# One whole gate column moved from behind the fourth pair of input products to between the second and the third

## The chip, the cores and the metric

The kernel runs on one core of one Trainium2 chip. The metric is the device time of one execution in microseconds (us); lower is better. Engines are called as the profile calls them: PE (TensorE, matrix products), DVE (VectorE), ACT (ScalarE), POOL (GpSimd), SP (SyncE, which here only issues DMAs).

## The reference, cut to what matters

One decoder layer over 1024 positions of width 1024, float32. `hybrid_mixer` is the part in which the change lies:

```python
def hybrid_mixer(u, w_in, conv_w, conv_norm_g, ret_norm_g, w_out):
    z = u @ w_in                                   # (1024, 1024) @ (1024, 3584)
    cb, cc, ch = jnp.split(z[..., :c0], 3, axis=-1)        # conv group, 512 channels each
    rq, rk, rv, rg = jnp.split(z[..., c0:], 4, axis=-1)    # retention, 4 heads x 128
    y_conv = cb * causal_dwconv3(cc * ch, conv_w)
    y_conv = group_rms_norm(y_conv, conv_norm_g, CONV_GROUPS)
    ...
    o = chunkwise_retention(q, k, v).reshape(b, s, RET_WIDTH)
    y_ret = group_rms_norm(o, ret_norm_g, RET_HEADS) * jax.nn.silu(rg)
    return jnp.concatenate([y_conv, y_ret], axis=-1) @ w_out

def reference(x, ...):
    h = h + hybrid_mixer(rms_norm(h, norm1_g), ...)
    h = h + sq_relu_mlp(rms_norm(h, norm2_g), w_up, w_down)
    return rms_norm(h, final_norm_g)
```

## The kernel before, in words

Channels lie on the partitions, positions on the free axis, in two halves of 512 (`hs`). Every float32 product is made of three products of rounded numbers: a weight piece `r` (128x512) is split into a high part `wh` (an ACT cast) and a low part `wl` (a subtraction on DVE or POOL), and an activation likewise into `uh`, `ul` (or `U`, `yh`, `yl`). One product of 128 output channels by 512 positions over 512 inputs is 12 matmuls (line 403, in `mm`).

`w_in` is worked through in column tiles of 128, numbered by `f`. 0 to 11 belong to the convolution (`f // 3` is its group of channels, `f % 3` is 0 for `cc`, 1 for `ch`, 2 for `cb`), 12 to 19 are the q and k columns, 20 to 23 the four gates `rg`, one for each head. The q and k tiles come first. Then `IN_TURNS` says in which turns the others are made, and `IN_END` which come last:

```python
IN_TURNS = [0, 1, 2, 3, 20, (4, 5), (6, 7), (8, 9), (10, 11), 21]
IN_END = [22, 23]
```

- A number is a *whole* turn (`whole`, by `tile_in`): two PSUM banks at once, one for each half, and 48 matmuls that alternate between the two banks. When they are done, DVE empties both; for a gate it multiplies by `R` (the norm of the row), ACT takes the Silu, and DVE multiplies by the head's output `o_n` (this is `gate`).
- A tuple is a *pair* (`pair_in`): two column tiles by both halves, made with seven products instead of eight (Strassen's scheme), in the order `UP_ORDER = (1, 2, 5, 6, 3, 7, 4)`, each 12 matmuls in one bank. Products 1, 2 and 3 read `uh`/`ul`, the others the sums `U`. Product 1 is copied out by ACT; DVE adds the others together: one add for product 2, two for 6, one for 3, two for 7, one for 4. The bank of product 5 is read by the second add of product 6 and again by that of 7. For each pair POOL or DVE also makes four sums of weight pieces (`r<-r,r`).
- `IN_END` makes gates 22 and 23 with four banks that are all taken at the start; the order is 22 first half, 23 first half, 22 second half, 23 second half, each 24 matmuls in one bank. The output product with `w_out` follows and reads `yh`, `yl` of all eight channel tiles.

There are 8 PSUM banks: four in the pool `pm` (whole turns, products 1, 5, 3, 4 of a pair, `IN_END`) and four in `pr` (products 2, 6, 7, and the norms). A bank goes to the next tile in the order in which they were given up. The banks of product 1 and of product 3 of a pair are the two that the next tiles of `pm` get.

Four result tiles (`o` of heads 2 and 3, `y` of groups 0 and 1) are stored to DRAM early (`put_by`, line 872) and fetched back (`get_back`, line 877) at a fixed place of the loop over `IN_TURNS`, line 894:

```python
    for at, turn in enumerate(IN_TURNS):
        if isinstance(turn, tuple):
            pair_in(turn)
        else:
            whole(turn)
        if at == len(IN_TURNS) - 2:
            for h in (2, 3):
                force(("by", ("o", h)))
                o_n[h, 0] = o_n[h, 1] = get_back(("o", h))
            for i in range(2):
                force(("by", ("y", i)))
                y[i] = get_back(("y", i))
```

The rest of the convolution and of the gates (`conv_h`, `conv_b`, `norm`, `gate`, `split_y`) runs as small tasks between the products. At the time of writing the program, a planner (`background`) keeps a clock for each engine from fixed costs (the class `Engine`, line 74 in the profile for all that it issues) and one `SLOT` of 2.72 us for every 12 matmuls; by these it decides behind which product a step is written and, where two engines could do it, whether POOL or DVE does. What it decides is fixed in the program; on the chip each engine works through its own list in order. `norm` of a convolution tile writes two matmuls into PE's list (lines 483 and 484), which read the tile `s` of ACT and that of DVE or POOL. Weight pieces are split four ahead (`prepare`, four buffers each of `r`, `wh` and `wl`): a new `wh` can be cast only when PE is done with the piece four before, and a new piece is fetched (line 162) only when the split of the one four before it has been done. So SP's list, on which all these fetches and line 877 stand, waits for the splits.

The MLP, which is two thirds of the time, comes behind all this and its code is not touched.

Of the kernel before, what the change touches and what calls it, by code (L numbers as in the profile page):

```python
# [36 lines left out]


IN_QK = [12, 13, 16, 17, 14, 15, 18, 19]
IN_TURNS = [0, 1, 2, 3, 20, (4, 5), (6, 7), (8, 9), (10, 11), 21]  # L40
IN_END = [22, 23]
SLOT, LOOK, PE_MARGIN, LATE = 2.72, 3.2, 1.2, 0.0
WARM = 10
# [36 lines left out]
def hybrid_layer(  # L80
# [107 lines left out]
    IN_ORDER = list(IN_QK)  # L188
    for turn in IN_TURNS + IN_END:
        IN_ORDER += turn if isinstance(turn, tuple) else [turn]  # L190
# [37 lines left out]
    ahead = 3  # L228
    for turn in IN_TURNS + IN_END:
        if isinstance(turn, tuple):  # L230
# [191 lines left out]
    def spawn(gen, ready=None, late=0.0):  # L422
        Task(gen, now[0] if ready is None else ready, late).go()
# [39 lines left out]
    def force(key):  # L463
        while key not in got:
            background(1e9)
            assert key in got, key
# [276 lines left out]
    def whole(f):  # L743
        def evac(z):
            if f < 20 and f % 3 == 0:
                out = a_of[f // 3] = unit(s="a")
                for half, sl in enumerate(hs):
                    act.copy(out[:, sl], z[half])
                return
            out = None if f < 20 and f % 3 == 1 else unit(s="z")  # L750
            for half in range(2):
                spawn(use(f, half, out, z[half], True), clock[dve])

        tile_in(evac)
# [68 lines left out]
    def pair_in(fs):  # L823
        out = [unit(s="z") for _ in range(2)]
        (c11, c12), (acc, c22) = ([o[:, sl] for sl in hs] for o in out)
        for at, n in enumerate(UP_ORDER):
            if not got.get("pairs") and n in (5, 6, 7, 4):
                for j in range(4):
                    force(({5: "t1", 6: "t2", 7: "t3", 4: "t4"}[n], j))
            b = product(n, (pm, pr)[at % 2])  # L830
            slot()
            prepare()
            ready = None
            if n == 1:
                act.copy(acc, b)
            if n == 2:
                dve.tensor_add(c11, acc, b)
                ready = 0, 0
            if n == 5:
                b5 = b  # L840
            if n in (6, 7, 4):
                dve.tensor_add(acc, acc, b)
            if n == 6:
                dve.tensor_add(c12, acc, b5)
            if n == 7:
                dve.tensor_add(c22, acc, b5)
                ready = 1, 1
            if n == 3:
                dve.tensor_add(c12, c12, b)
                ready = 0, 1  # L850
            if n == 4:
                ready = 1, 0
            if ready:
                f, half, o = fs[ready[0]], ready[1], out[ready[0]]
                if f < 20 and f % 3 == 0:
                    a_of[f // 3] = o
                else:
                    spawn(use(f, half, o, o[:, hs[half]], False), clock[dve], LATE * half)
            tick()
        got["pairs"] = now[0]  # L860
# [5 lines left out]
    def put_by(key, of, *ready):  # L866
        for r in ready:
            yield r
        yield (dve,)
        t = of()  # L870
        spilt[key] = spill.tile([P, T], F32, tag="sp", name=nm("sp"))
        nc.sync.dma_start(spilt[key], t)
        mark(("by", key), dve)

    def get_back(key):
        t = unit(s="back")
        nc.sync.dma_start(t, spilt.pop(key))
        return t
# [13 lines left out]
    for i in range(2):  # L892
        spawn(put_by(("y", i), lambda i=i: y[i], ("y", i, 0), ("y", i, 1)))
    for at, turn in enumerate(IN_TURNS):
        if isinstance(turn, tuple):
            pair_in(turn)
        else:
            whole(turn)
        if at == len(IN_TURNS) - 2:
            for h in (2, 3):  # L900
                force(("by", ("o", h)))
                o_n[h, 0] = o_n[h, 1] = get_back(("o", h))
# [3 lines that stand above are left out]
                got["back", i] = now[0] + 10.0  # L906
# [656 lines left out]
```

## Time and profile before

| | before |
|---|---|
| device time, median of 3 runs (lowest to highest) | 1080.27 us (1080.08 to 1080.79) |
| the profiled execution's own time | 1081.81 us |
| its span | 1079.0 us |
| mean granted clock of PE | 0.997 |
| busy share of the span: PE, DVE, ACT, POOL | 98%, 81%, 43%, 50% |

The span is the time from the first to the last instruction that the profile holds. The times in a timeline are microseconds from the span's start. A number in brackets at the end of a timeline's row is the idle time of that engine ahead of the row, and what ended it; the profile gives all engine instructions that the planner issues the line of its helper, L74, so they are told apart by the names of their tiles.

### The profile page before, as it was taken

The page shows a single profiled execution, that of the slowest core. Times are in us where ns is not written, and L with a number is a line of the kernel's source. Part 1 is how long each engine was busy: PE and PEld are TensorE (multiplying, and loading weights), DVE is VectorE, ACT ScalarE, POOL GpSimd, SP SyncE. Part 2 cuts the span into 40 slices and gives each one's busy share as a digit, 9 for nine tenths or more (in the row PEclk, how much of TensorE's full clock was granted, in tenths as well). Part 3 has the DMA queues.
Part 4 walks back from the last instruction along what each step waited for, and adds up shares of the span by engine and source line. Part 5 has one row for each costly group of instructions (what it writes and reads, how often), then busy time and mean ns, then how long its engine had stood idle before and what let it go on. Part 6 is the DMA issues. An engine that isn't in the chain of part 4 may idle for free.

```text
span 1079.0 us, 13854 instructions
## 1 busy us (share of the span) xinstructions
PE 1060.5 (98%) x4860; PEld 881.6 (82%) x4860; DVE 878.7 (81%) x1246; ACT 460.2 (43%) x904; POOL 538.0 (50%) x366
## 2 busy tenths in 40 slices
PE   9999999999989999999999999999999999999997
PEld 7888888887768888788788888888888888888886
DVE  7446546799998656699999989989899899899955
ACT  8211445663435544444433443433343344334453
POOL 6234223255753223559538358267276185384552
PEclk9999999999999999999999999999999999999999
DMA  7111122222223635050121211201301301200204
GB/s 274 62 59 39 40 70 78 75 79 73 78 59 118 215 104 188 1 195 21 48 88 39 69 49 49 79 30 57 90 21 50 98 20 50 88 20 20 69 30 156
DMA packets 39685, 82.25 MB, mean 76 GB/s; under 512 B 4544, under 2 KB 5696, under 8 KB 39616
## 3 DMA queue, kind: packets, MB, share of 16 engines
q1 hardware_dynamic: 39328, 80.85, 23.0%
q8 instruction: 38, 0.62, 0.2%
q10 hardware_dynamic: 288, 0.52, 0.1%
q14 instruction: 31, 0.25, 0.1%
HBM read 71.92 MB, written 9.44 MB: 75 GB/s over the span
## 4 chain that ended last, share of the span: by engine, by line
PE 79%; DVE 10%; POOL 4%; issue 3%; ACT 2%; DMA 1%; DVEq 0%; SPq 0%; POOLq 0%; ACTq 0%
PE b L403 46%; PE b L1276 22%; PE b L357 4%; PE b L1385 4%; DVE wl L74 2%; DVE z L74 2%; POOL z L74 1%; POOL r L74 1%; DVE t L74 1%; DVE x L74 1%; DVE U L74 1%; DVE q L74 1%; DVE xs L74 1%; ACT h L74 1%; DVE m L74 1%
## 5 line engine op out<-in xcount | busy, mean ns | idle before, releaser
L403 PE MATMUL b<-U,wh 128*128 128x512 f32 x1024 | 315.8, 390 | 1.8 <-DVE x L74 1.1
L74 ACT CAST wh<-r 128x512 fp32r<-128x512 f32 x286 | 175.9, 620 | 321.2 <-PE b L403 134.5
L74 DVE TENSOR_TENSOR wl<-r,wh 128x512 fp32r<-128x512 f32 x251 | 231.8, 926 | 91.4 <-ACT wh L74 90.5
L74 POOL TENSOR_TENSOR r<-r,r 128x512 f32<-128x512 f32 x136 | 209.9, 1546 | 116.3 <-DVE wl L74 65.6
L1276 PE MATMUL b<-V,wh 128*128 128x512 f32 x784 | 242.0, 389 | 0.5 <-POOL V L74 0.4
L403 PEld LDWEIGHTS b<-U,wh 128*128 128x128 f32 x1024 | 191.8, 188 | 42.6 <-issue 1.9
L74 DVE TENSOR_TENSOR x<-x,b 128x512 f32<-128x512 f32 (+1 forms) x312 | 195.6, 673 | 30.2 <-PE b L1385 14.2
L403 PE MATMUL b<-U,wl 128*128 128x512 f32 x512 | 199.5, 390 | 0.3 <-POOL wl L74 0.3
L1276 PEld LDWEIGHTS b<-V,wh 128*128 128x128 f32 x784 | 147.1, 188 | 32.3 <-POOL V L74 0.8
L74 POOL TENSOR_TENSOR t<-t,t 128x512 f32<-128x512 f32 x70 | 106.4, 1524 | 97.9 <-ACT t L74 51.9
L1276 PE MATMUL b<-V,wl 128*128 128x512 f32 x392 | 152.5, 389 | 0.0
L74 POOL TENSOR_TENSOR wl<-r,wh 128x512 fp32r<-128x512 f32 x35 | 48.6, 1394 | 160.7 <-ACT wh L74 153.5
L403 PEld LDWEIGHTS b<-U,wl 128*128 128x128 f32 x512 | 96.2, 188 | 21.2 <-POOL wl L74 0.7
L403 PE MATMUL b<-uh,wh 128*128 128x512 f32 x304 | 103.4, 399 | 2.3 <-DVE z L74 2.3
L403 PE MATMUL b<-uh,wl 128*128 128x512 f32 x304 | 100.8, 391 | 1.1 <-DVE wl L74 1.1
L403 PE MATMUL b<-ul,wh 128*128 128x512 f32 x304 | 101.0, 392 | 0.0
L1276 PEld LDWEIGHTS b<-V,wl 128*128 128x128 f32 x392 | 73.5, 188 | 15.2
L74 POOL TENSOR_TENSOR V<-t,V 128x512 fp32r<-128x512 f32 x35 | 49.6, 1416 | 67.3 <-ACT V L74 67.3
L74 DVE TENSOR_TENSOR t<-t,b 128x512 f32<-128x512 f32 x112 | 75.8, 677 | 1.7 <-POOL t L74 1.2
L74 ACT ACTIVATE t<-t 128x512 f32<-128x512 f32 x64 | 40.2, 631 | 79.8 <-DVE t L74 79.2
L74 DVE TENSOR_TENSOR V<-t,V 128x512 fp32r<-128x512 f32 x63 | 70.3, 1116 | 0.0
L403 PEld LDWEIGHTS b<-uh,wl 128*128 128x128 f32 x304 | 57.3, 189 | 13.9 <-DVE wl L74 1.5
(178 smaller groups left out, 1422.1 us busy)
## 6 DMA issues: line engine op xcount, KB each, us to landing
r<-w_up_t SPq DMA_DIRECT2D x64, 256.0 KB, 2.6
r<-w_down_t SPq DMA_DIRECT2D x56, 256.0 KB, 2.7
r<-w_in_t SPq DMA_DIRECT2D x48, 256.0 KB, 2.7
xt<-xT SPq DMA_DIRECT2D x16, 256.0 KB, 5.4
xs<-xT SPq DMA_DIRECT2D x8, 512.0 KB, 4.9
r<-w_out_t SPq DMA_DIRECT2D x16, 256.0 KB, 2.7
x<-xT SPq DMA_DIRECT2D x8, 512.0 KB, 8.9
k<-x SPq DMA_DIRECT2D x6, 512.0 KB, 3.2
```

The source lines that it names most:

```text
L74: return f(out, *args, **kw)
L357: nc.tensor.matmul(vb[i], a[k][:, i * P : (i + 1) * P], b[k // 2][:, vs], start=(k == 0 and a is uh and b is vh), stop=(k == KT - 1 and a ...
L403: nc.tensor.matmul(b, a[:, k, :], rhs(n, k)[r], start=(start and i == 0), stop=(stop and i == len(ops) - 1),)
L1276: nc.tensor.matmul(b, a, r, start=(i == 0), stop=(i == len(ops) - 1))
L1385: nc.tensor.matmul(z, a, b, start=(k == 0 and t == 0), stop=(k == 3 and t == 2))
```

## The change

Gate column 21 is made right behind the pair (6, 7), ahead of (8, 9). The number of turns is the same, and the weights are fetched in the new order. The fetch from DRAM still stands behind the pair (10, 11), which is now the last turn, and `IN_END` follows it directly.

```diff
-IN_TURNS = [0, 1, 2, 3, 20, (4, 5), (6, 7), (8, 9), (10, 11), 21]
+IN_TURNS = [0, 1, 2, 3, 20, (4, 5), (6, 7), 21, (8, 9), (10, 11)]
...
-        if at == len(IN_TURNS) - 2:
+        if at == len(IN_TURNS) - 1:
             for h in (2, 3):
                 force(("by", ("o", h)))
                 o_n[h, 0] = o_n[h, 1] = get_back(("o", h))
```

The planner decides anew from there on. What stands in the lists of the engines at three places, before and after, follows. In these rows a name's number tells tiles apart: `b` is a PSUM bank's tile, `z` and `a` are result tiles, `cv` the convolution, `q_617` and `q_618` the outputs of heads 0 and 1.

PE, the turn that follows the pair (10, 11), before: `b_2860` is product 4 of the pair, `b_2895` and `b_2896` are the two banks of the whole turn 21, and the second of them had belonged to product 3 of the pair.

```order
L403 MATMUL b_2860<-U_2224,wh_2774 128x512 x2
L403 MATMUL b_2860<-U_2224,wl_2775 128x512
L403 MATMUL b_2895<-uh_157,wh_2807 128x512
L403 MATMUL b_2896<-uh_157,wh_2807 128x512
L403 MATMUL b_2895<-ul_165,wh_2807 128x512
```

And after: `b_2929` is product 4 of the same pair, and `b_2965` the first bank of `IN_END`, which had belonged to product 1 of that pair.

```order
L403 MATMUL b_2929<-U_2224,wh_2843 128x512 x2
L403 MATMUL b_2929<-U_2224,wl_2844 128x512
L403 MATMUL b_2965<-uh_157,wh_2876 128x512
L403 MATMUL b_2965<-ul_165,wh_2876 128x512
L403 MATMUL b_2965<-uh_157,wl_2877 128x512
```

Two banks within two instructions have become one; the next one (`b_2968`, formerly product 3) is asked for 24 matmuls later. Behind the pair (6, 7) the whole turn 21 now asks for two at once.

DVE, the stretch behind the last add of the pair (6, 7) (the first row of each), before, where the pair (8, 9) follows:

```order
L74 TENSOR_TENSOR z_2361<-z_2361,b_2512 128x512
L74 SCALAR_TENSOR_TENSOR r_2486<-b_2478,r_2486 128x512
L74 TENSOR_TENSOR wl_2551<-r_2379,wh_2550 128x512
L74 SCALAR_TENSOR_TENSOR z_2200<-z_2200,less_g,r_2485 128x512
L74 SCALAR_TENSOR_TENSOR z_2200<-r_2486,z_2200 128x512
L74 TENSOR_TENSOR wl_2575<-r_2405,wh_2574 128x512
L74 TENSOR_TENSOR z_2535<-z_2536,b_2561 128x512
```

And after, where the whole turn 21 (`z_2610` and the two `q_618`) stands between:

```order
L74 TENSOR_TENSOR z_2361<-z_2361,b_2516 128x512
L74 TENSOR_TENSOR z_2360<-z_2360,ssq 128x512
L74 TENSOR_TENSOR z_2360<-z_2360,z_2361 128x512
L74 SCALAR_TENSOR_TENSOR cv_2556<-z_2360,sm,cv_2556 128x512 x2
L74 SCALAR_TENSOR_TENSOR cv_2556<-z_2360,sm,cv_2556 128x511
L74 SCALAR_TENSOR_TENSOR cv_2556<-z_2360,sm,cv_2556 128x510
L74 TENSOR_TENSOR z_2610<-b_2540,R 128x512
L74 TENSOR_TENSOR z_2610<-b_2541,R 128x512
L74 SCALAR_TENSOR_TENSOR q_618<-z_2610,sm,q_618 128x512 x2
L74 TENSOR_TENSOR wl_2653<-r_2448,wh_2652 128x512
L74 TENSOR_TENSOR z_2617<-z_2618,b_2639 128x512
```

The convolution of group 2 (`cv`), which stood among the adds of the pair (8, 9), now stands ahead of them, in the time of turn 21; three of its four products that POOL made are DVE's now (two of them are the same row twice and shown once).

SP, around the four fetches from DRAM (`back`), before:

```order
L162 DMA r_2851<-w_out_t 128x512
L162 DMA r_2873<-w_out_t 128x512
L877 DMA back_2887<-sp_1991 128x1024
L877 DMA back_2889<-sp_1993 128x1024
L877 DMA back_2891<-sp_2221 128x1024
L877 DMA back_2893<-sp_2584 128x1024
L162 DMA r_2929<-w_out_t 128x512
```

And after:

```order
L162 DMA r_2920<-w_out_t 128x512
L162 DMA r_2942<-w_out_t 128x512
L877 DMA back_2956<-sp_1991 128x1024
L877 DMA back_2958<-sp_1993 128x1024
L877 DMA back_2960<-sp_2221 128x1024
L877 DMA back_2962<-sp_2537 128x1024
L162 DMA r_3084<-w_out_t 128x512
```

They stood behind the second piece of `w_out`, whose buffer had held the second piece of gate 22. They now stand behind the fourth, whose buffer held the second piece of gate 23. On ACT, the Silu and the reciprocal root of the norm belong to different tables: before, one change of table stands between the pair (10, 11) and the end of `IN_END`; after, three stand there.

## The prediction

> **What bounds the kernel now.** I read the page first, then the busy time in stretches around the change, then the timelines of PE, DVE, ACT and SP there.
>
> ```profile
> span 1079.0 us, 13854 instructions
> PE 1060.5 (98%) x4860; PEld 881.6 (82%) x4860; DVE 878.7 (81%) x1246; ACT 460.2 (43%) x904; POOL 538.0 (50%) x366
> PE 79%; DVE 10%; POOL 4%; issue 3%; ACT 2%; DMA 1%; DVEq 0%; SPq 0%; POOLq 0%; ACTq 0%
> ```
>
> PE is busy for 98%, and PE's own work makes 79% of the chain that ended last. The change leaves the number of matmuls as it is, so it can only win or lose PE's idle or slowed time. The stretches below are cut at PE's borders: pair (6, 7); pair (8, 9) with a norm; pair (10, 11) with a norm; turn 21 with two norms; `IN_END`.
>
> ```profile
> core 0: us, PE busy (x) PEld busy (x) DVE busy (x) ACT busy (x) POOL busy (x), PEclk, DMA share, GB/s
> 254.41:276.66 22.25, 20.91 (x90) 16.36 (x88) 20.98 (x22) 11.77 (x19) 15.52 (x11) 1.00 0.17 48
> 276.66:298.23 21.57, 20.36 (x87) 15.99 (x86) 21.23 (x23) 6.75 (x12) 14.75 (x10) 1.00 0.23 73
> 298.23:318.36 20.13, 19.80 (x87) 16.06 (x86) 18.93 (x20) 8.64 (x15) 14.29 (x10) 1.00 0.21 60
> 318.36:334.26 15.90, 13.59 (x53) 10.81 (x52) 12.61 (x18) 5.65 (x10) 4.34 (x3) 0.89 0.50 171
> 334.26:356.02 21.76, 21.76 (x97) 18.02 (x96) 17.50 (x23) 12.38 (x22) 6.52 (x4) 1.00 0.17 53
> ```
>
> `IN_END` has 96 matmuls in 21.76 us and nothing to wait for: 0.2267 us each. At that pace a pair (84) takes 19.04, turn 21 (48) 10.88, a norm (2) 0.45. So the four stretches lose: pair (6, 7), with two norms, 22.25 - 19.95 = 2.30; pair (8, 9) 21.57 - 19.49 = 2.08; pair (10, 11) 20.13 - 19.49 = 0.64; turn 21 15.90 - 11.79 = 4.11. What the change can reach is the last three: 6.8 us. In two of the four DVE is busy nearly throughout (20.98 of 22.25, 21.23 of 21.57).
>
> ```profile
> 267.03 0.50 PE L403 MATMUL b<-uh,wl 128*128 128x512 f32 x1 [1.12 <-DVE wl L74]
> ...
> 295.80 0.40 PE L403 MATMUL b<-U,wl 128*128 128x512 f32 x1
> 297.17 0.50 PE L483 MATMUL b<-s,blkr 128*128 128x512 f32 x1 [0.97 <-ACT s L74]
> 297.89 0.50 PE L484 MATMUL b<-s,blkr 128*128 128x512 f32 x1 [0.23 <-DVE s L74]
> ...
> 307.13 0.50 PE L484 MATMUL b<-s,blkr 128*128 128x512 f32 x1 [0.33 <-DVE r L74]
> ...
> 318.36 0.39 PE L403 MATMUL b<-uh,wh 128*128 128x512 f32 x1
> 321.06 0.79 PE L403 MATMUL b<-uh,wh 128*128 128x512 f32 x1 [2.31 <-DVE z L74]
> 321.65 1.05 PE L403 MATMUL b<-ul,wh 128*128 128x512 f32 x2
> ...
> 324.21 0.69 PE L403 MATMUL b<-ul,wh 128*128 128x512 f32 x2
> ```
>
> The 4.11 have two parts. Turn 21's second matmul, into its second bank, starts 321.06 - 318.36 - 0.23 = 2.47 us late, behind an add of DVE. Then seven matmuls take 324.21 - 321.06 = 3.15 us in place of 1.59: a slow clock (0.89 over the stretch) that costs 1.56.
>
> ```profile
> 272.44 2.19 DVE L74 TENSOR_TENSOR z<-z,b 128x512 f32<-128x512 f32 x3
> ...
> 281.94 0.68 DVE L74 TENSOR_TENSOR z<-z,b 128x512 f32<-128x512 f32 x1
> ...
> 283.14 0.68 DVE L74 TENSOR_TENSOR wl<-r,wh 128x512 fp32r<-128x512 f32 x1
> ...
> 287.13 1.77 DVE L74 TENSOR_TENSOR wl<-r,wh 128x512 fp32r<-128x512 f32 x1
> ...
> 318.82 2.19 DVE L74 TENSOR_TENSOR z<-z,b 128x512 f32<-128x512 f32 x3
> ...
> 327.66 0.68 DVE L74 TENSOR_TENSOR z<-z,b 128x512 f32<-128x512 f32 x1
> ```
>
> I call it DVE's lag how long after a pair's end on PE its last add (of product 4) begins. Behind (6, 7) it is 281.94 - 276.66 = 5.3 us, behind (10, 11) 327.66 - 318.36 = 9.3. The third add of the row at 318.82 is that of product 3, whose bank turn 21 gets: it ends at 321.01, and PE goes on at 321.06. The lag is the cause.
>
> ```profile
> L74 ACT CAST wh<-r 128x512 fp32r<-128x512 f32 x286 | 175.9, 620 | 321.2 <-PE b L403 134.5
> ...
> L74 POOL TENSOR_TENSOR r<-r,r 128x512 f32<-128x512 f32 x136 | 209.9, 1546 | 116.3 <-DVE wl L74 65.6
> ...
> L74 POOL TENSOR_TENSOR wl<-r,wh 128x512 fp32r<-128x512 f32 x35 | 48.6, 1394 | 160.7 <-ACT wh L74 153.5
> ```
>
> **The change part by part.** *The bank wait goes (2.47 and 1.56).* Behind (6, 7) turn 21 asks for the same pair of banks, but the add of product 3 there is the third of the row at 272.44 and done by 274.63, 2.0 us before PE arrives at 276.66; up to it the lists of PE and DVE hold the same work. `IN_END` asks for one bank (product 1, emptied by ACT long before) and for the next (product 3) only 24 matmuls, 5.4 us, later. With a lag up to 9 that is in time. Both terms to nought: 4.0, with the rest of the stretch 4.11.
>
> *The waits in the two pairs (2.08 and 0.64).* They hang on the lag. From the last add of (6, 7) to that of (10, 11) DVE had 46 instructions in 327.66 - 281.94 = 45.72 us, 0.994 each. After, it has 50 between the same two adds (the evacuation and the gate of 21 come in, four; three of POOL's products; others went to POOL). PE needs 10.88 + 2 x 19.49 = 49.86 for what lies between. At the old mean 50 take 49.7: the lag stays at 5.1 and no longer grows. That is one bound. For the other I went through the new lists by hand, 0.6 us (start to start) for an instruction of DVE that reads a bank or runs while POOL rests, 1.7 for one that meets POOL's (the two `wl` rows show both), 1.3 to 1.7 for one of POOL (rows of the page, above; their means are 1.39 and 1.55), 0.62 for a cast of ACT. The last add of (6, 7) comes at 282.9, since three SBUF instructions meet POOL; the banks of 21 are emptied by 292.7, its Silu done by 293.4, behind which ACT has the `wh` of product 3 of (8, 9), whose `wl` POOL then ends at 295.4 (PE comes for it at 298.9); the `s` tile for the first norm at 300.8 (PE: 303.9); the lag is 4.5 behind (8, 9) and 1.8 behind (10, 11). No wait of PE is left on that walk. So these two stretches keep between 0 and 2.72, the latter if they wait as before, and up to 4.6 if both do as (6, 7) did, with a lag like the first bound. I take 0.8, near the walk, whose margins are 3 us.
>
> *The end of the mixer (nothing, from below nothing to 4 us).* Turn 21 no longer covers what follows the last pair: 15.90 us less between the last pair and `w_out`. By the new list the norm of the last group stands 48 matmuls behind the pair (10.9 us), its two halves of `y` and the four tiles from DRAM must be split before `w_out`.
>
> ```profile
> 327.26 1.85 SPq L877 DMA_DIRECT2D back<-sp x4
> ...
> DMA to landing us min/median/max: 3.7/7.0/8.2
> ```
>
> ```profile
> 331.62 0.69 DVE L74 TENSOR_TENSOR s<-t,s 128x512 fp32r<-128x512 f32 x1 [0.64 <-ACT s L74]
> ```
>
> ```profile
> 334.01 0.69 ACT L74 ACTIVATE r<-b,eps 128x512 f32<-128x512 f32 x1 [0.24 <-PE b L484]
> ...
> 335.98 0.64 ACT L74 ACTIVATE r<-r 128x512 f32<-128x512 f32 x1
> 336.63 1.28 ACT L74 ACT_TABLE_LOAD   x1
> 337.93 1.15 ACT L74 ACTIVATE z<-z 128x512 f32<-128x512 f32 x2
> ```
>
> From the pair's end: the split of gate 23's second piece waits for product 4 and takes a cast and 1.7 of POOL, so SP goes on at 2.4; it issues one piece and the four fetches by 4.8; they land by 4.8 + 8.2 = 13.0. ACT's list then holds the cast of the last fetched tile (0.6), a table (1.28), four roots (2.6), a table (1.28), a Silu and the first `wh` of `w_out` (0.6 each): 20.0. POOL's `wl` is done at 21.3. PE, with `IN_END` (21.76) and two norms (0.9), asks for it at 23.1. Margin 1.8 us: cost nothing, and what lies beyond the margin would be paid one for one. The norm's own `s` is ready 332.31 - 327.66 = 4.65 behind the last add, so with a lag below 6.2 PE doesn't wait there either.
>
> The Trainium skill, "ScalarE: Activation LUTs", What ACT_TABLE_LOAD costs, speaks against the change: it puts a switch of table at 2.66 us, a load of 1.28 and a drain of 1.38. Here the load is 1.28 and its neighbours stand 0.02 us off, so no drain shows. By the page the two switches would add 2.8 us to that list, 1.0 beyond the margin, and the time would be 1075.3 (an estimate).
>
> *The rest of SP's list* (the `x` tiles, line 942) stands relative to the end of `IN_END` as before, and the MLP's lists are unchanged; it is only moved ahead.
>
> **Sum.** 4.11 + 2.72 - 0.8 = 6.0 us: span 1079.0 to 1073.0, that execution's own 1081.81 to 1075.8. It lay 1.5 above the median, so on the median 1080.27 - 6.0 = 1074.3.
>
> **The rivals.**
> *A, the pairs go on waiting.* For it: (6, 7) lost 2.30 with a lag of 5.3 at its end; the average holds 5.1. Then 4.11 is won and up to 4.6 - 2.72 = 1.9 of it given back: 1076.2 to 1078.1. Against it: the walk.
> *B, the slow clock isn't the wait's doing* but falls somewhere anyway: 1.56 stays, 1075.8. The waits of 1.12 and 0.97 were followed by no slow matmuls, the one of 2.31 was, which speaks against it. The Trainium skill, "TensorE: Matmul & The Clock Gate", What's actually happening, has the clock fall after an idle window of some 3.4 us; 2.31 is less, so by that rule B would stand.
> *C, the wait moves to the start of `w_out`.* If the fetches go out as late behind the last pair as before (327.26 - 318.36 = 8.9 in place of 2.8), they land at 18.9, the first `wl` is done at 27.3, PE waits 4.2 and pays the slow clock, 1.56, too: 0.2 won, 1080.1. Against it: SP waited then for splits that stood behind 9 us of lag.
> *D, DVE falls further behind, slower.* It got four more instructions, and among them three of POOL's. If the lag behind (10, 11) reached 12, the norm's `s` would be ready at 16.7, PE waiting 5.8 in `IN_END`, with 1.56 of slow clock and the 2.72 of the pairs as before: 10.1 lost against 6.8, 1083.5. It is slower by over 0.2% from a lag of 11 on. Against it: 10.88 more PE time for four more instructions.
>
> **How the numbers follow.** 0.2% (2.2 us) is about what a measurement here can tell from no change. The forecast (0 to 1.8 us kept, 1073.4 to 1075.3): 0.60; A 0.14; B 0.05; C 0.11; D 0.10. Faster is the forecast, A and B, 0.79; the same 0.11; slower 0.10. The best is all 6.8 and the scatter of the runs, 0.5: 1072.9; the upper end is A's worst, 1078.1; C and D, 0.21, lie beyond, and some of C (a wait of 2 us, 1076) within.
>
> **What would show it.** In the profile after: no wait of PE for an add at the start of a turn from 276 to 350; a granted clock of 1.00 there; DVE's last add within 5 us of the end of (10, 11); the four fetches issued within 5 us of it; `w_out` begun at about 350 in place of 356.02. The prediction is wrong if PE waits for `s` in `IN_END`, for `wl` at the first matmul of `w_out`, or if DVE's lag is above 6 at the end of the last pair.

## The result, and the profile after

| | before | after |
|---|---|---|
| median of the runs shown with the changed kernel (4 and 4) | 1080.17 us | 1072.45 us |
| ratio, with its 95% interval | | 0.994 (0.9926 to 0.9953) |
| median of the repetition (23 and 6 runs) | 1078.94 us | 1072.87 us |
| ratio, with its 95% interval | | 0.9943 (0.993 to 0.9957) |
| the profiled execution's span and own time | 1079.0, 1081.81 us | 1070.6, 1073.52 us |

The change makes the kernel 6.1 us faster by the repetition, which has the most runs of before; the first comparison gave 7.7. The forecast was 6.0 us, 1074.3 against 1080.27; the first median, 1072.45, lies even under the best that the prediction named, 1072.9.

The page of the kernel after: the span, the busy time of the engines, the chain that ended last by engine.

```profile
span 1070.6 us, 13856 instructions
PE 1056.1 (99%) x4860; PEld 879.3 (82%) x4860; DVE 877.7 (82%) x1249; ACT 465.3 (43%) x908; POOL 534.0 (50%) x363
PE 90%; DVE 5%; issue 1%; ACT 1%; POOL 1%; DMA 0%; DVEq 0%; SPq 0%; ACTq 0%; POOLq 0%
```

PE has the same 4860 matmuls; its share of the chain rose from 79% to 90%, DVE's fell from 10% to 5%. The stretches, cut at PE's borders in the new order: pair (6, 7); turn 21; pair (8, 9) with a norm; pair (10, 11) with a norm; `IN_END` with two norms.

```profile
core 0: us, PE busy (x) PEld busy (x) DVE busy (x) ACT busy (x) POOL busy (x), PEclk, DMA share, GB/s
251.91:274.24 22.33, 20.92 (x90) 16.36 (x88) 21.03 (x24) 11.79 (x19) 14.34 (x10) 1.00 0.23 71
274.24:285.12 10.88, 10.88 (x50) 9.01 (x48) 10.66 (x11) 2.78 (x5) 7.97 (x6) 1.00 0.12 48
285.12:304.61 19.49, 19.49 (x87) 16.14 (x86) 17.10 (x19) 10.28 (x16) 12.18 (x9) 1.00 0.16 55
304.61:324.10 19.49, 19.49 (x87) 16.14 (x86) 17.73 (x23) 7.82 (x14) 8.94 (x7) 1.00 0.27 81
324.10:346.77 22.67, 22.67 (x101) 18.77 (x100) 19.69 (x28) 16.39 (x26) 5.15 (x4) 1.00 0.33 117
```

Four of the five lose nothing: PE is busy for the whole of each, and 10.88, 19.49, 19.49 and 22.67 (21.76 and two norms, 0.91) are the lengths that the prediction had worked out for stretches without a wait. The clock is 1.00 throughout. Only (6, 7) keeps its loss, 22.33 - 19.95 = 2.38 us. The end of the mixer, on DVE (the last add and the norm's `s`), SP, POOL, PE and ACT:

```profile
328.75 0.68 DVE L74 TENSOR_TENSOR z<-z,b 128x512 f32<-128x512 f32 x1
...
332.71 0.69 DVE L74 TENSOR_TENSOR s<-t,s 128x512 fp32r<-128x512 f32 x1
```

```profile
328.35 2.07 SPq L877 DMA_DIRECT2D back<-sp  x4
```

```profile
344.58 1.48 POOL L74 TENSOR_TENSOR wl<-r,wh 128x512 fp32r<-128x512 f32 x1 [16.64 <-ACT wh L74]
```

```profile
334.98 0.39 PE L483 MATMUL b<-s,blkr 128*128 128x512 f32 x1
...
335.66 0.39 PE L484 MATMUL b<-s,blkr 128*128 128x512 f32 x1
...
346.77 0.39 PE L403 MATMUL b<-yh,wh 128*128 128x512 f32 x1
...
347.22 0.39 PE L403 MATMUL b<-yh,wl 128*128 128x512 f32 x1
```

```profile
333.74 1.28 ACT L74 ACT_TABLE_LOAD   x1
...
338.17 1.28 ACT L74 ACT_TABLE_LOAD   x1
...
341.42 0.63 ACT L74 ACTIVATE r<-r 128x512 f32<-128x512 f32 x1
342.07 1.28 ACT L74 ACT_TABLE_LOAD   x1
343.36 0.63 ACT L74 ACTIVATE z<-z 128x512 f32<-128x512 f32 x1
```

The lag behind (10, 11) is 328.75 - 324.10 = 4.65 us. The norms' four matmuls begin at 334.98; the last tile `s` that they need, DVE's for the second half, is ready at 333.40, and the fourth of them (L484) takes it at 335.66: 2.3 us to spare. The first `wl` of `w_out` is done at 344.58 + 1.48 = 346.06, PE takes it at 347.22: 1.2 us to spare.

**Where the 8.4 us between the two first traces lie.** Both have the same matmul of (6, 7) behind a wait for `wl` (at 267.03 before, quoted in the prediction), and the first matmul of `w_out`. With the two further traces of before and one of after that were taken below:

| | before, 1st | before, 2nd | before, 3rd | after, 1st | after, 2nd |
|---|---|---|---|---|---|
| start of the span to that matmul | 267.03 | 264.53 | 264.73 | 264.61 | 264.33 |
| from it to the first of `w_out` | 88.99 | 87.32 | 88.89 | 82.16 | 82.17 |
| from there to the end of the span | 722.9 | 723.8 | 723.3 | 723.9 | 724.0 |

The change's part is the middle row: 88.99 - 82.16 = 6.8 us. The 2.4 us ahead of it are not the change's, since two other traces of before start as those of after do. Most of them lie in the first microseconds: in the first 12 us of the span PE does 36 matmuls in the first trace of before, 45 and 44 in the other two, and 46 and 48 in those of after. The trace of `bank` below, 38 matmuls, starts as late. The MLP (last row) gives back 0.0 to 1.0 us, within what it varies from trace to trace.

### The profile page after: what moved, and what is told of

It reads as the page before. It is cut to its first block, busy times and chain, and to the rows that moved or that the text cites. A ratio compares the mean times of both kernels' runs of the same rounds, so it can differ in the third digit from the quotient of the medians.

```text
span 1070.6 us, 13856 instructions
## 1 busy us (share of the span) xinstructions
PE 1056.1 (99%) x4860; PEld 879.3 (82%) x4860; DVE 877.7 (82%) x1249; ACT 465.3 (43%) x908; POOL 534.0 (50%) x363
## 4 chain that ended last, share of the span: by engine, by line
PE 90%; DVE 5%; issue 1%; ACT 1%; POOL 1%; DMA 0%; DVEq 0%; SPq 0%; ACTq 0%; POOLq 0%
PE b L403 56%; PE b L1276 23%; PE b L357 4%; PE b L1385 4%; DVE wl L74 1%; DVE t L74 1%; DVE x L74 1%; DVE q L74 1%; PE b L339 0%; DVE V L74 0%; PE b L625 0%; PE b L595 0%; ACT h L74 0%; PE b L663 0%; PE b L627 0%
## 5 line engine op out<-in xcount | busy, mean ns | idle before, releaser
L74 DVE TENSOR_TENSOR wl<-r,wh 128x512 fp32r<-128x512 f32 x247 | 227.2, 922 | 86.3 <-ACT wh L74 85.6
L74 POOL TENSOR_TENSOR wl<-r,wh 128x512 fp32r<-128x512 f32 x39 | 56.3, 1448 | 166.3 <-ACT wh L74 158.8
```

What stands on the lines that cost most here:

```text
L74: return f(out, *args, **kw)
```

## The experiments

The theory is the prediction's: DVE's lag behind PE at a pair's end makes all these waits, and a whole turn, which gives DVE little to do for 10.9 us of PE, makes the lag up if it stands between the pairs. The rival: turn 21 behind the last pair asked for two banks at once, one of them product 3's, and that request alone was the cost. "Stretch" is the middle row of the table above.

| run | edit | median us | against before | stretch | lag behind (10, 11) |
|---|---|---|---|---|---|
| after_again | the changed kernel | 1072.87 | 0.9943 (0.993 to 0.9957) | 82.17 | 4.63 |
| bank | before, other bank | 1078.60 | 0.9994 (0.9985 to 1.0003) | 87.33 | 9.27 |
| relief | before, DVE less | 1075.18 | 0.9963 (0.9949 to 0.9977) | 84.67 | 7.57 |
| first | 21 behind (4, 5) | 1078.32 | 0.9994 (0.9984 to 1.0003) | | 8.03 |
| third | 21 behind (8, 9) | 1075.26 | 0.9963 (0.995 to 0.9977) | 84.31 | 4.72 |
| half | after, 7 adds more | 1077.05 | 0.998 (0.997 to 0.9991) | 84.47 | 8.56 |
| load | after, 14 adds more | 1080.19 | 1.0012 (1.0003 to 1.0021) | 89.38 | 11.82 |
| early | after, fetches earlier | 1073.01 | 0.9941 (0.9923 to 0.9959) | 82.18 | 5.22 |
| twenty | after, 20 behind (4, 5) | 1083.69 | 1.0046 (1.0033 to 1.006) | | 3.85 |

The runs were made in three groups, on three chips, and before ran beside each: 1078.94 us (after_again, bank, first, third), 1079.17 (relief, load, twenty) and 1079.14 (half, early). A comparison across groups is good to about these 0.2 us. `first` and `twenty` have no entry under stretch, since their matmuls come in another order there. The changed kernel again, without an edit:

> The changed kernel once more, to see what of its gain is the change's. In the two profiles shown so far the span fell by 8.4 us, of which 6.8 lie in the mixer and 2.4 ahead of the first difference in any list (the first matmuls start 0.6 us earlier and run faster). Theory 1: those 2.4 us are a scatter of the start, met by both kernels; the span from the same matmul to the same matmul behind the change (from the pair (6, 7)'s begin to the first matmul of w_out) falls by 6.8 again, and the medians differ by 6 to 8 us. Theory 2: the start differs from kernel to kernel; then this run starts like the first run of the changed kernel and the kernel before like its first run, and they are again 8 us apart.

The second trace of after starts as late as the first (264.33 and 264.61) and has the same stretch. The medians differ by 6.1 us, and the start is a scatter that before has too: theory 1.

**bank.** The kernel before, with the second bank of turn 21 from the other pool.

```diff
-    def tile_in(evac):
+    def tile_in(evac, second=None):
...
-        out = [bank() for _ in hs]
+        out = [bank(), bank(second)]
...
-        tile_in(evac)
+        tile_in(evac, pr if f == 21 else None)
```

> The kernel before with nothing moved: the second bank of turn 21 is taken from the other pool, so that it is not the one of product 3 of the pair (10, 11). The lists of all engines keep their order. Theory 1 (the wait of turn 21 is the wait for that bank, and the slow clock is its consequence): 2.31 us of wait and 1.56 of slow matmuls go, the stretch of turn 21 falls from 15.9 to 11.9 us, the waits in the pairs (8, 9) and (10, 11) stay; 4.0 us faster, 0.9963 of before. Theory 2 (DVE's lag of 9 us holds PE up wherever it comes next): PE waits at the next place instead, for product 3's bank in the gates 22 and 23 or for s of the norm, and less than 1 us is won. Theory 3 (the slow clock is not the wait's doing): 2.4 us faster, with a granted clock below 0.95 somewhere between 316 and 334.

It won nothing that can be measured: 0.3 us, in an interval that holds no change. The stretch of turn 21 in this kernel, and the matmuls of the norms behind it:

```profile
317.41:331.72 14.31, 12.87 (x53) 9.68 (x52) 12.17 (x18) 5.37 (x10) 3.57 (x3) 1.00 0.45 139
```

```profile
329.33 0.49 PE L483 MATMUL b<-s,blkr 128*128 128x512 f32 x1 [0.87 <-ACT s L74]
330.05 0.49 PE L484 MATMUL b<-s,blkr 128*128 128x512 f32 x1 [0.23 <-DVE s L74]
330.66 0.50 PE L483 MATMUL b<-s,blkr 128*128 128x512 f32 x1
331.38 0.50 PE L484 MATMUL b<-s,blkr 128*128 128x512 f32 x1 [0.22 <-DVE s L74]
```

The wait for the bank is gone, and the four matmuls of the norms, which lose nothing in the kernel before, now take 331.72 - 327.84 - 0.45 (the two matmuls at 327.84) - 4 x 0.2267 = 2.5 us more than their work. The stretch is 14.31 against 14.42 us in a run of before without slow matmuls (below). So theory 2: the lag, 9.27 us as before, holds PE up at the next place where it needs DVE. The request for two banks decided only where PE waited.

**relief.** Before, with less for DVE to do: this kernel leaves out the second and third tap of the convolution of groups 2 and 3, so its result is not the layer's.

```diff
-        for j in (1, 2):
+        for j in (1, 2) if i < 2 else ():
```

> The kernel before, order of turns unchanged, with less work for DVE: the second and third tap of the convolution are left out for the groups 2 and 3 (eight products of DVE; six of them, 2.44 + 1.52 + 2.46 us busy and 1.6 us of waiting for ACT around them, stand ahead of the add for which turn 21 waits). Theory 1 (the waits come from DVE's lag): the lag behind (10, 11) falls from 9.3 to below 5, the wait at turn 21's second bank goes although the same bank is asked for, with the slow matmuls, and the waits in (8, 9) and (10, 11) go or halve: 4 to 6 us faster. Theory 2 (the request of two banks at once behind a pair makes the wait): at least 1.5 us of the wait at turn 21 stays, and the gain is below 2 us.

The gain is 4.0 us, at the lower end; 87.32 - 84.67 = 2.65 of it is in the stretch, against the trace of before without slow matmuls. The planner, seeing DVE free, gave it other work: two products of the convolution now stand ahead of the pair's last add, from 318.11 to 321.64, and the lag fell to 7.57 only, not below 5. The granted clocks of its four runs are 0.998 and 0.999, so the slow clock is gone too (see the third trace of before, below). The wait fell with the lag, and of the waits in (8, 9) and (10, 11) one of 0.22 us is left. Product 3's add and the matmul that waits for it:

```profile
313.11 2.19 DVE L74 TENSOR_TENSOR z<-z,b 128x512 f32<-128x512 f32 x3
```

```profile
315.36 0.50 PE L403 MATMUL b<-uh,wh 128*128 128x512 f32 x1 [0.98 <-DVE z L74]
```

The lag is 1.75 us shorter than in the second trace of before (9.32) and the wait 1.35 shorter (2.33 there), with the same request for the same bank. Theory 2 kept at least 1.5 of it and a gain below 2; neither is so.

**first.** Whole gate 21 one pair earlier than in the changed kernel.

```diff
-IN_TURNS = [0, 1, 2, 3, 20, (4, 5), (6, 7), 21, (8, 9), (10, 11)]
+IN_TURNS = [0, 1, 2, 3, 20, (4, 5), 21, (6, 7), (8, 9), (10, 11)]
```

> Whole gate 21 one pair earlier still, behind (4, 5), so that three pairs follow in a row. Before, DVE's lag behind (4, 5) is 7.4 us (last add at 261.82, the pair's end at 254.41) and the wait of 2.3 us in (6, 7) follows. Theory 1 (DVE's lag at a pair's start decides; a whole turn of 10.9 us makes it up): the wait in (6, 7) goes too, 2.3 us; turn 21 itself waits 0.3 for product 3's bank. The lag then grows over three pairs, and if it is over 7 behind (10, 11) PE waits at the last norm and at w_out: between 2 us faster and 2 us slower than the changed kernel, whose lag is 4.65 there. Theory 2 (only the request of two banks at once behind the last pair mattered, and the waits in the pairs are made by the weights' pieces): the wait in (6, 7) stays and the time is that of the changed kernel within 0.5 us.

It is 5.5 us slower than the changed kernel, outside what either theory allowed. The wait of (6, 7) for `wl` did go, but PE waits for `s` of norms (0.71, and 1.50 in (8, 9)), and three pairs in a row bring the lag to 8.03. At the end PE then waits for the norm and for `w_out`:

```profile
302.82 0.51 PE L483 MATMUL b<-s,blkr 128*128 128x512 f32 x1 [1.50 <-ACT s L74]
...
338.04 0.50 PE L484 MATMUL b<-s,blkr 128*128 128x512 f32 x1 [0.63 <-DVE s L74]
...
351.52 0.50 PE L403 MATMUL b<-yh,wl 128*128 128x512 f32 x1 [0.79 <-POOL wl L74]
```

The direction is theory 1's (the lag grew, and above 7 the end is late), its size was taken too small. No bank is asked for in a hurry at the end of this kernel either.

**third.** Whole gate 21 one pair later than in the changed kernel.

```diff
-IN_TURNS = [0, 1, 2, 3, 20, (4, 5), (6, 7), 21, (8, 9), (10, 11)]
+IN_TURNS = [0, 1, 2, 3, 20, (4, 5), (6, 7), (8, 9), 21, (10, 11)]
```

> Whole gate 21 one pair later than in the changed kernel, between (8, 9) and (10, 11). Theory 1 (the lag at a pair's start decides): (8, 9) follows (6, 7) as before and keeps its 2.08 us; the add of product 3 of (8, 9) ended at 298.4 before, when PE was done with the pair at 298.2, so turn 21 waits about 0.2 us; (10, 11) has no wait. 4.5 us faster than before, 2.3 slower than the changed kernel. Theory 2 (the waits in the pairs don't hang on the lag): like the changed kernel within 0.5 us.

It is 2.4 us slower than the changed kernel by the medians, 84.31 - 82.17 = 2.1 by the stretches, as theory 1 said (2.3). (8, 9) waits as before; turn 21 behind it does not, and neither does (10, 11):

```profile
293.91 0.49 PE L483 MATMUL b<-s,blkr 128*128 128x512 f32 x1 [0.99 <-ACT s L74]
294.64 0.50 PE L484 MATMUL b<-s,blkr 128*128 128x512 f32 x1 [0.23 <-DVE s L74]
```

**load** and **half.** The changed kernel with work added to DVE, 14 adds and 7, and in both one add more at the end, which uses the result (it is zero, so the kernel's result stays). The edit of `load`; `half` has `fs[0] >= 10` in place of `fs[0] >= 8`:

```diff
+    scratch = xp.tile([P, 2 * P], F32, tag="h", name=nm("h"), bufs=6)
+    nc.vector.memset(scratch, 0.0)
...
+            if fs[0] >= 8:
+                nc.vector.tensor_add(scratch, scratch, scratch)
...
+            if n == 4 and fs[0] == 10:
+                nc.vector.tensor_add(acc[:, : 2 * P], acc[:, : 2 * P], scratch)
```

> The changed kernel with more work for DVE: one more add of 128x256 for each product of the pairs (8, 9) and (10, 11), 14 in all, which the planner doesn't count. At 0.4 to 0.9 us each they take 6 to 12 us, and DVE is idle for 2.39 + 1.76 us in the two pairs. Theory 1 (the lag decides): the lag behind (10, 11) grows from 4.65 to 7 to 12 us, PE waits in the gates 22 and 23 for s of the norm as soon as it is over 6.9, and at the first products of w_out for wl: 1 to 6 us slower than the changed kernel, though no bank is asked for in a hurry. Theory 2 (only the request of two banks at once mattered): within 0.5 us of the changed kernel.

> As the run with 14 more adds on DVE, but only the seven in the pair (10, 11). At 0.4 to 0.9 us each they are 2.8 to 6.3 us, and DVE is idle for 1.76 us in that pair: the lag of 4.65 grows to between 5.7 and 9.2. Theory 1 (a threshold: PE waits at the norm's s only from a lag of 6.2 to 6.9 on, and loses nothing below): 0 to 3 us slower than the changed kernel, by about the part of the lag that lies above 6.5, and no wait of PE inside the pair. Theory 2 (every us of DVE's lag costs, since the tail of the mixer is a chain from DVE): 2 to 4.5 us slower.

With 14 adds the lag is 11.82 us and the kernel 7.3 us slower than the changed one (1080.19 against 1072.87), more than the 1 to 6 expected. PE waits for `s` of the norm, where theory 1 put it, and slow matmuls follow, 0.43 us each in place of 0.23. Ahead of that it waits for `wh` and `wl` in `IN_END` (1.8 us), which neither theory had; at the first products of `w_out`, where theory 1 expected a wait, there is none:

```profile
338.35 0.50 PE L483 MATMUL b<-s,blkr 128*128 128x512 f32 x1 [2.05 <-ACT s L74]
339.57 0.50 PE L484 MATMUL b<-s,blkr 128*128 128x512 f32 x1 [0.72 <-DVE s L74]
...
340.85 0.63 PE L403 MATMUL b<-uh,wh 128*128 128x512 f32 x1
341.28 0.63 PE L403 MATMUL b<-ul,wh 128*128 128x512 f32 x1
```

With seven the lag is 8.56 and the loss 4.0 us against the run of the changed kernel with earlier fetches beside it (1077.05 and 1073.01). That is outside the 0 to 3 of theory 1 and within theory 2's range:

```profile
336.23 0.50 PE L483 MATMUL b<-s,blkr 128*128 128x512 f32 x1 [0.63 <-ACT s L74]
337.45 0.50 PE L484 MATMUL b<-s,blkr 128*128 128x512 f32 x1 [0.72 <-DVE s L74]
350.94 0.50 PE L403 MATMUL b<-yh,wl 128*128 128x512 f32 x1 [0.78 <-POOL wl L74]
```

The stretch up to `w_out` is 84.47 - 82.17 = 2.3 us longer, which is about the 2.1 us of lag above 6.5 that theory 1 gave; what it left out is `w_out`, which waits as well, behind the norm, and loses 1.5 us more there. The pair itself has no wait. That a lag behind (10, 11) costs nothing up to 5.2 (the run with earlier fetches, below) and 2.3 us and more from 8 on is shown; whether the edge lies at 6.9, where the trace of after puts it (4.65 and the 2.3 us that the last `s` has to spare), no run tells: of the kernels that end as the changed one does, none has a lag between 5.2 and 8.0. Against theory 2, that every us costs, speaks the run with earlier fetches: 0.6 us more lag without a loss. For the rival these two runs are the end: nothing in them asks for banks otherwise than in the changed kernel, and they lose 4 and 7 us.

**early.** The fetches from DRAM one turn earlier.

```diff
-        if at == len(IN_TURNS) - 1:
+        if at == len(IN_TURNS) - 2:
```

> The changed kernel with the four fetches from DRAM one turn earlier, behind (8, 9). Theory 1 (the end of the mixer has a margin, 1.3 us at the first wl of w_out): no difference, within 0.5 us of the changed kernel; the fetches land some 15 us earlier and their splits move ahead. Theory 2 (splits that come earlier fall into DVE's busy time in (10, 11) and raise its lag): up to 1 us slower.

No difference: 1073.01 against 1072.87 us, the stretch 82.18. The fetches are issued at 309.60 in place of 328.35. The lag rises by 0.6, to 5.22, as theory 2 had it, and costs nothing at that size.

**twenty.** Gate 20 moved as well, to behind (4, 5).

```diff
-IN_TURNS = [0, 1, 2, 3, 20, (4, 5), (6, 7), 21, (8, 9), (10, 11)]
+IN_TURNS = [0, 1, 2, 3, (4, 5), 20, (6, 7), 21, (8, 9), (10, 11)]
```

> The changed kernel with whole gate 20 moved too, from ahead of the pair (4, 5) to behind it, so that a whole turn follows each of the first two pairs. The pair (6, 7) still loses 2.38 us in the changed kernel, with a lag of 7.4 us behind (4, 5). Theory 1 (a whole turn makes up the lag wherever it stands): the loss of (6, 7) falls below 0.7 and the time by 1.5 to 2.3 us against the changed kernel. Theory 2 (the sums U of the inputs, which DVE makes until 225, and which the pair (4, 5) needs 10.9 us earlier now, are late): PE waits for U in (4, 5), 1 to 5 us slower than the changed kernel.

What both theories describe came about, and the second weighs more than expected: 10.8 us slower than the changed kernel, where it had 1 to 5. The two rows of PE, and the stretches (pair (4, 5) from its last matmul ahead of the wait up to 246; all that follows up to `w_out`):

```profile
235.93 0.80 PE L403 MATMUL b<-U,wh 128*128 128x512 f32 x1 [6.28 <-ACT U L74]
240.22 0.79 PE L403 MATMUL b<-U,wh 128*128 128x512 f32 x1 [3.49 <-DVE U L74]
```

```profile
229.26:246.00 16.74, 6.97 (x19) 4.88 (x18) 12.76 (x16) 6.23 (x9) 8.71 (x6) 0.69 0.33 128
246.00:357.14 111.14, 111.14 (x493) 92.00 (x492) 90.88 (x108) 54.60 (x84) 52.99 (x37) 1.00 0.23 72
```

PE waits 6.28 and 3.49 us for `U`, and the granted clock of that stretch is 0.69. Behind that it is busy for 111.14 of 111.14 us: the loss of (6, 7), the last one left, is gone. The 2.4 us are there to be had, at a price of some 13.

**before_again** and **before_third.** The kernel before, for its trace.

> The kernel before once more, for its trace. On this chip its spans lie between 1074.7 and 1077.4, with granted clocks of 0.998 and of 0.996 to 0.997, against 1079.0 at 0.997 in the trace read for the prediction. Theory 1 (the cost of the wait at turn 21 differs from run to run, since the slow clock follows it in some runs only): a span of about 1075 has the wait of 2.3 us without slow matmuls behind it, one of about 1077 has them. Theory 2 (it is the start and the MLP that differ): the stretch of turn 21 is 15.9 us again, and the difference lies ahead of 250 or behind 356.

> The kernel before a third time, for its trace: the waits of 2.3 us at turn 21 were followed by slow matmuls in the first trace (1.56 us) and by none in the second. Theory 1 (the slow clock follows that wait in a part of the runs): the wait is 2.3 again, the matmuls behind it slow or not, and the stretch of turn 21 with two norms is 15.9 or 14.3 us. Theory 2 (the first trace had something else): 14.3 again, and a span above 1076 comes from the start.

Turn 21 with its norms, in the second trace and in the third:

```profile
315.64:330.06 14.42, 12.10 (x53) 9.65 (x52) 12.27 (x18) 5.43 (x10) 3.63 (x3) 1.00 0.48 157
```

```profile
315.89:331.86 15.97, 13.70 (x53) 10.82 (x52) 12.57 (x18) 5.65 (x10) 4.33 (x3) 0.89 0.51 188
```

And the wait for the bank in each, with what follows:

```profile
318.35 0.50 PE L403 MATMUL b<-uh,wh 128*128 128x512 f32 x1 [2.33 <-DVE z L74]
318.69 0.63 PE L403 MATMUL b<-ul,wh 128*128 128x512 f32 x2
```

```profile
318.55 0.50 PE L403 MATMUL b<-uh,wh 128*128 128x512 f32 x1 [2.27 <-DVE z L74]
318.89 0.63 PE L403 MATMUL b<-ul,wh 128*128 128x512 f32 x2
319.36 0.76 PE L403 MATMUL b<-uh,wl 128*128 128x512 f32 x2
319.91 1.05 PE L403 MATMUL b<-uh,wh 128*128 128x512 f32 x2
```

The wait is 2.33 and 2.27 us. In the second trace the clock stays at 1.00 behind it; in the third the slow matmuls come, as in the first, but not at once: the third row has the first of them. Theory 1: the wait is always there, the slow clock follows in some runs, and the stretch is 14.4 or 16.0 us. How often, the granted clocks of the single runs tell: the four traces with slow matmuls in the middle have 0.994 to 0.997 over the span, the nine without them 0.998 or 0.999, and of the 23 runs of before 12 have 0.996 or 0.997 (median span 1076.8 us) and 11 have 0.998 (1075.1). The six of after have 0.998 or 0.999.

## Why the prediction was right

*The cause, DVE's lag: shown.* `relief` took load off DVE in the old order and won 4.0 us; `load` and `half` put it on in the new one and lost 7.3 and 4.0; `bank` took the request away and left the lag, and won nothing.

*The bank wait, 2.47, with 1.56 of slow clock.* Gone, as forecast. But the 1.56 is not in every run of before: two of three traces have it, and by the granted clock 12 of 23 runs. The steady part of the gain is 87.32 - 82.16 = 5.2 us, and 6.7 to 6.8 with the slow clock. The medians, 6.1 us apart, lie between; 5.2 + 1.55 x 12/23 would be 6.0 (an estimate).

*The pairs, 2.72, of which 0.8 was kept back: mis-sized.* (8, 9) and (10, 11) keep nothing. The walk through the lists, which had found no wait, was right here and the bound from (6, 7) too cautious. The walk's own lags were too short: the last add of (6, 7) came 280.76 - 274.24 = 6.5 us behind the pair (walk 6.2), and behind (10, 11) the lag is 4.65 (walk 1.8, average pace 5.1). So the average was nearer for the lag, and the walk for the waits: a lag of 4.65 doesn't reach PE.

*The end of the mixer, nothing.* Right, with a smaller margin: 1.2 us at the first `wl` of `w_out`, not 1.8. The four fetches began 4.25 us behind the pair and were issued by 6.3, not by 4.8, so that sign (within 5 us) was missed. At the norm the margin was larger than the prediction read it: the `s` that is ready 4.65 behind the last add is the second half's, which PE takes 0.68 us behind its first norm matmul, so the lag that PE can stand there is 6.9, not 6.2.

*The sum.* 6.0 us came from two terms that were each off: 0.8 too little in the pairs, and a slow clock counted in full that comes in about half of the runs, some 0.8 too much. That the two cancel is luck. The predicted median, 1074.3, was 1.9 above the first one measured: 1.3 because it started from three runs of before that all lay in the upper part of its scatter (1080.08 to 1080.79; later medians are 1078.94 to 1079.17), the rest within the scatter of the changed kernel (1072.45 and 1072.87). `w_out` began at 346.77, not 350: 2.4 of that is the late start of the first trace of before.

*Rival A* (the pairs go on waiting) and *B* (the slow clock falls elsewhere) didn't come: no stretch from 274 to 347 loses anything, at a clock of 1.00. The Trainium skill, "TensorE: Matmul & The Clock Gate", What's actually happening, spoke for B with an idle window of about 3.4 us; the traces show slow matmuls behind idle times of 2.27 and 2.31 us, and the measurement decides. That section of the Trainium skill also calls the window free-running, so that where in it work lands varies from run to run. The traces agree: the clock changes on a beat of 3.41 us, and the one trace of three without slow matmuls has its pause split over two beats (worked out in the last section).

*Rival C* (the wait moves to `w_out`) is real from a longer lag on: `first` and `half` wait there, 0.79 and 0.78 us, at lags of 8.03 and 8.56, and lose 1.5 us by it. `load`, with 11.82, doesn't: PE had by then lost 7.2 us at other places.

*Rival D* (DVE falls further behind) was priced at 5.8 + 1.56 = 7.4 us at a lag of 12, without the pairs. `load`, with 11.82, lost 7.3, but the terms differ: 3.8 in the norms' four matmuls, 1.5 of slow clock, and 1.8 in waits for `wh` and `wl` in `IN_END`, which the price had left out. That the sums agree is luck. What spoke against D, that 10.88 us of PE time stand against four instructions, was borne out.

*The table loads.* All three loads that now stand in front of `w_out` take 1.28 us, and the neighbours of the last are 0.02 and 0.01 us off. With the 2.66 of the Trainium skill, "ScalarE: Activation LUTs", What ACT_TABLE_LOAD costs, each would have taken 1.38 more and the margin would have been overrun (an estimate); it was not.

## What to carry to other kernels

When one engine trails another and the leader stalls at a buffer, giving it another buffer can just move the stall to the next thing that it needs from the trailing engine, as it did here: measure the lag, and see where it is made up. A block of work that is light for the trailing engine is best put between the heavy ones, as early as it is needed and no earlier than its operands allow: here one place later cost 2.4 us, one earlier 5.5, and moving a second block drew out a wait of 10 us for its neighbour's operands. And take more than one trace of the kernel before ahead of pricing a stall: its aftermath may be there in some runs only.

## What the runs showed of the hardware

- The granted clock changes on a fixed beat. The matmuls reach their full pace 10.34 us into the first trace of before and 6.32 us into the second, and in each of the 13 traces every later change of the clock lies a whole number of times 3.413 us behind that moment: 10.34 + 91 x 3.413 = 320.9 is where the slow clock of the first trace begins. Each slow stretch in the middle is one such beat at 0.50, or three in a row (`twenty`). One slow beat costs 1.5 to 1.6 us here. In the 13 traces it comes exactly when PE is idle for 2.0 us or more of the beat ahead of it, so the length of a single pause does not settle it. In the first and the third trace of before, the pause of turn 21 lies almost whole within one beat, PE is busy for 1.21 and 1.14 of its 3.41 us, and the next is slow. In the second trace the pause of 2.33 us is split: 0.9 us fall into one beat, 1.43 into the next, in which PE is busy for 1.98, and the clock stays. In `load`, pauses of 2.05 and 0.72 us leave 1.42 busy in one beat, and the next is slow. The most idle beat that no slow one followed has 1.6 us (`first`, 1.80 busy), the least idle one that a slow one followed has 2.0 (`load`); between them no trace tells. The beat with the pause and the next in the first trace of before, then the one with 1.43 us in the second:

```profile
317.54:320.95 3.41, 1.21 (x6) 0.67 (x4) 3.27 (x4) 0.00 (x0) 0.81 (x1) 1.00 0.54 154
320.95:324.36 3.41, 3.30 (x8) 2.62 (x9) 2.51 (x5) 1.75 (x3) 0.56 (x1) 0.50 0.00 0
```

```profile
316.92:320.33 3.41, 1.98 (x9) 1.64 (x10) 2.66 (x4) 0.54 (x1) 0.00 (x0) 1.00 0.20 63
```

- The runs of before lie between 1077.11 and 1081.04 us (23 runs), those of after between 1072.47 and 1073.99 (6). That this scatter is the one long pause's alone is not shown: `bank`, with no pause above 0.87 us near turn 21, lies between 1077.06 and 1080.29 (12 runs), and 5 of its runs have a granted clock of 0.997, though its trace has no slow beat. Two waits close together can fill a beat too, as in `load`; what did so in those five runs no trace shows.
- Of the 14 added DVE adds of 128x256 in `load`, the nine that began while POOL rested took 0.41 to 0.42 us, and the five that began while POOL worked on SBUF tiles 1.50 to 1.52. Together they took 11.3 us, of which 7.2 are left as lag.

```profile
297.59 0.42 DVE L838 TENSOR_TENSOR h<-h 128x256 f32<-128x256 f32 x1
...
299.63 1.52 DVE L838 TENSOR_TENSOR h<-h 128x256 f32<-128x256 f32 x1
```

```profile
299.59 1.29 POOL L74 TENSOR_TENSOR wl<-r,wh 128x512 fp32r<-128x512 f32 x1 [4.85 <-ACT wh L74]
```
